# Hybrid decoder block on one core: first feature groups with a pinned first chain, norm products ahead, the prompt's scale and shift on ACT, seven PSUM banks, a third split pair and one group's splits on POOL

## The chip, the core and the metric

The kernel runs on one core of a Trainium2 chip. A core has a matmul engine (TensorE, PE, with its weight loads as PEld), a vector engine (VectorE, DVE), an activation engine (ScalarE, ACT), a general engine (GpSimd, POOL) and a queue engine (SyncE, SP) that issues transfers. The metric is the device time of one execution in microseconds (us); lower is better. A figure for a kernel is the median of its runs.

## The reference

One layer of a decoder for a prompt of 256 tokens and for 8 requests of 4 tokens (288 columns in all), 2048 features wide, in float32:

```python
def block(x, c, st_pool, st_conv, st_ssm, st_ffn, pos0, lp):
    mod = silu(c) @ lp['w_ada'] + lp['b_ada']
    sh1, sc1, g1, sh2, sc2, g2 = split(mod, 6)
    h = rmsnorm(x, lp['norm1']) * (1 + sc1) + sh1
    proj = h @ lp['w_in']
    u_pool, z, xbc, dt_raw = split(proj)
    pool_out, new_pool = pool_mixer(u_pool, st_pool, pos0, lp['pool_w'], lp['pool_scale'])
    ssd_out, new_conv, new_ssm = ssd_mixer(z, xbc, dt_raw, st_conv, st_ssm, ...)
    mix = concatenate([pool_out, ssd_out]) @ lp['w_out']
    x = x + g1 * mix
    h2 = rmsnorm(x, lp['norm2']) * (1 + sc2) + sh2
    ffn_out, new_ffn = conv_ffn(h2, st_ffn, lp['w_up'], lp['ffn_conv_w'], lp['ffn_conv_b'], lp['w_down'])
    return x + g2 * ffn_out, new_pool, new_conv, new_ssm, new_ffn
```

`pool_mixer` averages over trailing windows, `ssd_mixer` is a depthwise convolution and a chunked state-space scan over 24 heads with a gated norm, `conv_ffn` is an MLP of width 5504 whose gate passes a short convolution. The outputs are both sets of tokens and the new states.

## The kernel before

Features lie on the partitions, tokens in the free dimension: a matmul has a 128 by 128 weight block and 288 columns. Each product in float32 is made of three matmuls (`mm3`, lines 235 to 237): weight hi by input hi, weight hi by input lo, weight lo by input hi. All weights stream in as tiles of up to 512 KB. `load` issues one on SP's queue into a slot of the tag "raw", waiting for a free one; `split` makes of it a pair of the tag "wsp": ACT casts the hi part (line 229), and DVE subtracts it from the raw tile for the lo part (line 230). The three rotating lists of slots are kept by `_W`: the pool w1 has RAW1 = 8 raws and SPLIT1 = 2 pairs for the whole kernel, and w0 adds RAW0 = 7 raws until the last feature group starts.

The input projection's 28 output tiles that are needed first (the scan's inputs, two pooling tiles and six tiles of z) are made not in one pass but in six passes over groups of features, since the features get ready one by one:

```python
KGROUPS = [(0, 1), (1, 1), (2, 2), (4, 4), (8, 4), (12, 4)]
```

Group gi has its first k-tile and the number of them. For each group there are three pieces of work. `ada_group_units(gi)` multiplies the conditioning by that group's columns of w_ada (tile adag, line 314, weights raw_ada), in as many visits as `VISIT` says: (raw tiles in a visit, output tiles of the group before at which the visits stand). It transposes the result (adat_g, line 329), adds the bias (ada, DVE, line 339) and makes the multiplier (amul, DVE, line 279). `modulate` makes the normalized input h_g: the product with the reciprocal norm rstd (DVE, line 377), scale and shift of the prompt's 256 columns (DVE, line 380), of the 32 sample columns (POOL, lines 385 and 386), then the hi part h1k by ACT (line 388) and the lo part by DVE (line 389). `xbc_units(gi)` runs the 28 tiles, each with 3 matmuls for every k-tile of the group, in one of 3 PSUM banks of the pool pm, and takes each bank out: group 0 by a copy of ACT (line 588), the later groups by an addition of DVE (line 590) to cvp, upp and ups, or zy. `MOD[gi]` says how many tiles before group gi's end the visits of the next group are finished and its `modulate` stands.

Each engine takes its instructions in the order that the program and its scheduler's priorities give; `split` and `modulate` have a high priority, so their instructions stand ahead of those written around them where nothing pins them. Behind the last group follow the dt product, the rest of the projection (uz, pool and z tiles) beside convolution, scan and norm of the mixer, the other parts of w_ada (adap, line 351), then the output projection, gate, value and down projection of the MLP.

## Time and profile before

| | |
|---|---|
| time, median of 3 runs | 1369.44 us (1365.91 to 1371.44) |
| profiled execution, its own time | 1371.33 us |
| its span | 1369.5 us |
| its mean granted TensorE clock | 0.992 |
| first matmul of groups 0, 1, 2, 3 | 21.77, 37.30, 56.80, 92.42 us |
| first matmul of the dt product, of uz, of the output projection | 202.25, 273.35, 392.24 us |
| DMA, mean over the span | 236 GB/s |

The page of a profile gives for each engine its busy time, share of the span and number of instructions. A row of the timeline has start and duration in us, engine, line, operation, output tile, input tiles and their shapes, the count where equal rows were joined, and in brackets the idle time ahead of it on its engine with what ended it. A row of a grouped view has the total busy time in us and the mean of one in ns. The span is the time between the profile's first and last instruction; the execution's own time is about 1.8 us longer.

### The profile page before, as it was taken

To read this page: it belongs to the slowest core of one execution; us is meant where nothing else is said; L and a number is where in the kernel's file an instruction comes from. 1 tells how busy PE (TensorE), PEld (TensorE's weight loads), DVE (VectorE), ACT (ScalarE), POOL (GpSimd) and SP (SyncE) were. 2 spreads that over 40 slices of the span, in tenths; PEclk is the share of its full clock that TensorE was granted. 3 is DMA by queue.
4 is the path that set the end of the run, shared out by engine and by line. 5 is a ranking of instruction groups with operands and counts; after the bars stand their busy time and mean duration, and the time that the engine had idled before them with its cause. 6 is when DMAs were issued, how large, how long until landed. Compare 5 with 4: busy or idle time off the path is not lost.

```text
span 1369.5 us, 26363 instructions
## 1 busy us (share of the span) xinstructions
PE 1338.9 (98%) x10565; PEld 1249.5 (91%) x10565; DVE 826.8 (60%) x1448; ACT 575.3 (42%) x925; POOL 230.4 (17%) x428
## 2 busy tenths in 40 slices
PE   9899999999989999999999999999999999999997
PEld 7788988777679898988999999999999999999997
DVE  3865667878674448654655455566565566566553
ACT  5322334388643334533443333444343334344442
POOL 0000000222222223111211001222120011122221
PEclk9999999999999999999999999999999999999998
DMA  9898796888878877788555555655555665556531
GB/s 376 344 349 309 270 338 258 299 292 310 306 300 318 314 268 260 239 284 289 198 187 183 162 177 189 197 188 190 186 176 164 188 195 185 192 199 188 185 119 69
DMA packets 97194, 323.20 MB, mean 236 GB/s; under 512 B 10736, under 2 KB 19888, under 8 KB 97072
## 3 DMA queue, kind: packets, MB, share of 16 engines
q1 hardware_dynamic: 93168, 310.63, 65.1%
q0 software_dynamic: 3184, 9.69, 1.9%
q8 instruction: 83, 1.36, 0.4%
q10 hardware_dynamic: 720, 1.19, 0.2%
q14 instruction: 39, 0.32, 0.1%
HBM read 309.78 MB, written 10.39 MB: 234 GB/s over the span
## 4 chain that ended last, share of the span: by engine, by line
PE 90%; DMA 4%; DVE 3%; ACT 1%; issue 0%; POOL 0%; SPq 0%; DVEq 0%; POOLq 0%; ACTq 0%
PE mm_down L236 7%; PE mm_down L237 7%; PE mm_down L235 7%; PE mm_val L236 6%; PE mm_gate L236 6%; PE mm_gate L235 6%; PE mm_gate L237 6%; PE mm_val L237 6%; PE mm_val L235 6%; PE xbc L235 4%; PE adap L351 4%; PE xbc L236 4%; PE xbc L237 4%; PE mm_out L235 3%; PE mm_out L236 2%; PE mm_out L237 2%
## 5 line engine op out<-in xcount | busy, mean ns | idle before, releaser
L236 PE MATMUL mm_down<-ahl,wsp_down 128*128 128x288 f32 x688 | 204.3, 297 | 0.0
L237 PE MATMUL mm_down<-ahl,wsp_down 128*128 128x288 f32 x688 | 202.8, 295 | 0.0
L235 PE MATMUL mm_down<-ahl,wsp_down 128*128 128x288 f32 x688 | 202.1, 294 | 0.0
L236 PE MATMUL mm_val<-h2k,wsp_val 128*128 128x288 f32 x640 | 190.1, 297 | 0.0
L236 PE MATMUL mm_gate<-h2k,wsp_gate 128*128 128x288 f32 x640 | 190.0, 297 | 0.0
L237 PE MATMUL mm_gate<-h2k,wsp_gate 128*128 128x288 f32 x640 | 188.8, 295 | 0.0
L237 PE MATMUL mm_val<-h2k,wsp_val 128*128 128x288 f32 x640 | 188.8, 295 | 0.0
L235 PE MATMUL mm_gate<-h2k,wsp_gate 128*128 128x288 f32 x640 | 188.8, 295 | 0.0
L235 PE MATMUL mm_val<-h2k,wsp_val 128*128 128x288 f32 x640 | 188.0, 294 | 0.0
L230 DVE TENSOR_TENSOR wsp_down<-raw_down,wsp_down 128x1024 fp32r<-128x1024 f32 x96 | 108.0, 1125 | 121.8 <-ACT wsp_down L229 121.8
L230 DVE TENSOR_TENSOR wsp_gate<-raw_gate,wsp_gate 128x1024 fp32r<-128x1024 f32 x80 | 98.1, 1228 | 136.2 <-ACT wsp_gate L229 136.1
L229 ACT CAST wsp_down<-raw_down 128x1024 fp32r<-128x1024 f32 x96 | 92.2, 960 | 167.3 <-PE mm_down L237 116.9
L229 ACT CAST wsp_gate<-raw_gate 128x1024 fp32r<-128x1024 f32 x80 | 83.9, 1050 | 160.4 <-PE mm_gate L237 69.0
L235 PE MATMUL xbc<-h1k,wsp_xbc 128*128 128x288 f32 x448 | 136.4, 306 | 8.9 <-DVE zy L590 4.0
L229 ACT CAST wsp_val<-raw_val 128x1024 fp32r<-128x1024 f32 x80 | 84.1, 1051 | 122.8 <-issue 103.7
L236 PE MATMUL xbc<-h1k,wsp_xbc 128*128 128x288 f32 x448 | 134.4, 300 | 0.9 <-DVE h1k L389 0.9
L237 PE MATMUL xbc<-h1k,wsp_xbc 128*128 128x288 f32 x448 | 132.7, 297 | 0.0
L235 PEld LDWEIGHTS mm_down<-ahl,wsp_down 128*128 128x128 f32 x688 | 129.6, 188 | 0.0
L236 PEld LDWEIGHTS mm_down<-ahl,wsp_down 128*128 128x128 f32 x688 | 129.3, 188 | 0.0
L237 PEld LDWEIGHTS mm_down<-ahl,wsp_down 128*128 128x128 f32 x688 | 129.2, 188 | 0.0
L235 PEld LDWEIGHTS mm_gate<-h2k,wsp_gate 128*128 128x128 f32 x640 | 120.5, 188 | 5.0 <-ACT ahl L1070 4.2
L235 PEld LDWEIGHTS mm_val<-h2k,wsp_val 128*128 128x128 f32 x640 | 120.6, 188 | 0.0
(316 smaller groups left out, 3000.5 us busy)
## 6 DMA issues: line engine op xcount, KB each, us to landing
raw_adap<-wflat SPq DMA_DIRECT2D x128, 512.0 KB, 5.9
raw_gate<-wflat SPq DMA_DIRECT2D x80, 512.0 KB, 3.5
raw_val<-wflat SPq DMA_DIRECT2D x80, 512.0 KB, 3.6
raw_ada<-wflat SPq DMA_DIRECT2D x64, 512.0 KB, 8.0
raw_xbc<-wflat SPq DMA_DIRECT2D x55, 512.0 KB, 8.6
raw_down<-wflat SPq DMA_DIRECT2D x48, 512.0 KB, 3.6
raw_out<-wflat SPq DMA_DIRECT2D x32, 512.0 KB, 6.4
raw_down<-wflat SPq DMA_DIRECT2D x32, 384.0 KB, 3.1
```

The costliest lines, as they stand in the source:

```text
L229: nc.scalar.copy(hi[:, :n], raw[:, a:a + n])
L230: nc.vector.tensor_tensor(lo[:, :n], raw[:, a:a + n], hi[:, :n].bitcast(F32), ALU.subtract)
L235: nc.tensor.matmul(ps, whi[:, w], bh, start=first, stop=False)
L236: nc.tensor.matmul(ps, whi[:, w], bl, start=False, stop=False)
L237: nc.tensor.matmul(ps, wlo[:, w], bh, start=False, stop=last)
L351: i = nc.tensor.matmul(ps[32 * j:32 * j + 32, :512], sc_c[:, k, :], raw[:, (j % 2) * 512:(j % 2) * 512 + 512], start=(k == ay - 1), stop=( ...
```

## The change

Eight things are changed together. (1) In group 0 the chain to the first h (line 339's add to line 389's lo part) is pinned in program order, and the split of the first xbc tile is written ahead of it; the second tile's split is written behind it, pinned as well. (2) The products with the norm are made in place on the x tiles, ahead: k-tile 0 and k-tiles 1 to 3 before the first chain, the other twelve in three instructions at tiles 4, 10 and 16 of group 0 (`normalize`). (3) `modulate1` makes the sample columns on DVE and the prompt's scale and shift with one ACT instruction for each k-tile. (4) In groups 0 to 4, four of every seven output tiles (m % 7 > 2) use a bank of the pool behind `aux`, which has four, so that the tiles run through seven banks. (5) In group 0 four of the 28 tiles (m % 7 == 5) are taken out by DVE. (6) RAW1 goes from 8 to 10 and RAW0 from 7 to 5, and w0 has a pair, so that there are three pairs until the last group starts; the raws are 15 as before until then, and 10 instead of 8 after it. (7) In group 1 POOL makes the lo parts of the splits. (8) Visits of group 3 come in four fours rather than two eights, MOD of groups 0 and 1 goes from 4 and 5 to 10 and 8, the load of vec moves from group 1 to group 3, and the scratch memory of DMAs with software descriptors is halved to 8192 bytes.

```diff
@@ -36,13 +36,13 @@
-RAW1, RAW2 = 8, 1
-RAW0 = 7
+RAW1, RAW2 = 10, 1
+RAW0, SPLIT0 = 5, 1
 SPLIT1, SPLIT2 = 2, 2
-PHASE = (192, 32, 0)
+PHASE = (192, 32, 0, 128)
 YK = 2
-VISIT = {1: (4, (10,)), 2: (4, (7, 15)), 3: (8, (8, 19)), 4: (8, (8, 19)), 5: (8, (8, 19))}
-MOD = (4, 5, 6, 6, 6)
+VISIT = {1: (4, (10,)), 2: (4, (7, 15)), 3: (4, (4, 9, 14, 19)), 4: (8, (8, 19)), 5: (8, (8, 19))}
+MOD = (10, 8, 6, 6, 6)
@@ -222,13 +222,24 @@
-    def split(raw, a, n, name):
+    kpo = tc.keep_in_program_order
+
+    def split(raw, a, n, name, eng=None, pin=False):
         pair = wp[0].tile([P, 2 * RAWC + 64], F32R, tag="wsp", name="wsp_" + name)
         hi, lo = pair[:, 0:RAWC], pair[:, RAWC + 32:2 * RAWC + 32]
         with tc.high_priority():
-            nc.scalar.copy(hi[:, :n], raw[:, a:a + n])
-            nc.vector.tensor_tensor(lo[:, :n], raw[:, a:a + n], hi[:, :n].bitcast(F32), ALU.subtract)
+            i = nc.scalar.copy(hi[:, :n], raw[:, a:a + n])
+            j = (eng or nc.vector).tensor_tensor(lo[:, :n], raw[:, a:a + n], hi[:, :n].bitcast(F32), ALU.subtract)
+        if pin:
+            kpo(i)
+            kpo(j)
         return hi, lo
+
+    def split_xbc(gi, ci, pin=False):
+        (ks, ms), key = _xbc_chunks(gi)[ci], ("xbc", gi, ci)
+        return ready.pop(key, None) or split(load(key), 0, len(ms) * len(ks) * P, f"xbc{gi}_{ci}",
+                                             nc.gpsimd if gi == 1 else None, pin)
+
 
     def mm3(ps, whi, wlo, c, bh, bl, first, last, n=P):
         w = slice(c * n, c * n + n)
...
@@ -323,8 +334,11 @@
             if gi:
                 yield
         r = 32 * nj
+        pin = kpo if gi == 0 else (lambda i: i)
+        if gi == 0:
+            ready[("xbc", 0, 0)] = split_xbc(0, 0, True)
         if gk == 1:
-            asb = ada_sb(ps, nb, f"g{gi}")
+            asb = ada_sb(ps, nb, f"g{gi}", pin=pin)
             pt = aux(f"adat_g{gi}")
             nc.tensor.matmul(pt[:, :r], asb[:, :nb], early[:, K_S2:K_S2 + r], start=True, stop=True)
             if gi == 0:
@@ -336,8 +350,8 @@
             o = ada[:, 0:2, k0:k0 + gk, :].rearrange("p a (b i) c -> p a b i c", b=nj // 2)[:, :, :, i, :]
             b = bada[:, 0:2, k0:k0 + gk].rearrange("p a (b i) -> p a b i", b=nj // 2)[:, :, :, i]
             src = pt[:, i * r:(i + 1) * r].rearrange("p (a b c) -> p a b c", a=2, b=nj // 2)[:, :, :, 0:NC9]
-            nc.vector.tensor_tensor(o, src, b.unsqueeze(3).to_broadcast([P, 2, nj // 2, NC9]), ALU.add)
-        ada_scale(0, 1, early[:, V_N1:V_N1 + KT], k0, gk)
+            pin(nc.vector.tensor_tensor(o, src, b.unsqueeze(3).to_broadcast([P, 2, nj // 2, NC9]), ALU.add))
+        pin(ada_scale(0, 1, early[:, V_N1:V_N1 + KT], k0, gk))
 
     def ada_part_units(part, ay=1):
         ps = pa.tile([P, 512], F32, tag="ada", name=f"adap{part}")
@@ -387,6 +401,29 @@
         for i in range(gk):
+
+    def normalize(k0, gk, r):
+        xv = xav(k0, gk)
+        kpo(nc.vector.tensor_tensor(xv, xv, r.unsqueeze(1).to_broadcast([P, gk, N]), ALU.mult))
+
+    def modulate1(k0, gk, name):
+
+        h = kp.tile([P, 4, N], F32, tag="hmod", name="h_" + name, bufs=2)
+        xv = xav(k0, gk)
+        pin = kpo if k0 == 0 else (lambda i: i)
+        with tc.high_priority():
+            hs = h[:, :gk, NP:N].rearrange("p k (b l) -> p k b l", b=NB)
+            xs = xv[:, :, NP:N].rearrange("p k (b l) -> p k b l", b=NB)
+            sa = amul[:, 0, k0:k0 + gk, 1:NC9].unsqueeze(3).to_broadcast([P, gk, NB, NL])
+            sb = ada[:, 0, k0:k0 + gk, 1:NC9].unsqueeze(3).to_broadcast([P, gk, NB, NL])
+            pin(nc.vector.tensor_tensor(hs, xs, sa, ALU.mult))
+            pin(nc.vector.tensor_tensor(hs, hs, sb, ALU.add))
+            for i in range(gk):
+                pin(nc.scalar.activation(h[:, i, 0:NP], xv[:, i, 0:NP], AF.Identity,
+                                         scale=amul[:, 0, k0 + i, 0:1], bias=ada[:, 0, k0 + i, 0:1]))
+                pin(nc.scalar.copy(xhi[0][k0 + i], h[:, i, :]))
+                pin(nc.vector.tensor_tensor(xlo[0][k0 + i], h[:, i, :], xhi[0][k0 + i].bitcast(F32), ALU.subtract))
 
 
     class _W:
@@ -569,9 +606,10 @@
     def xbc_units(gi):
         k0, gk = KGROUPS[gi]
         for ci, (ks, ms) in enumerate(_xbc_chunks(gi)):
-            hi, lo = split(load(("xbc", gi, ci)), 0, len(ms) * gk * P, f"xbc{gi}_{ci}")
+            hi, lo = split_xbc(gi, ci)
             for b, m in enumerate(ms):
-                ps = pm.tile([P, 512], F32, tag="mm", name=f"xbc{gi}_{m}")
+                wide = gi < len(KGROUPS) - 1 and m % 7 > 2
+                ps = aux(f"xbc{gi}_{m}") if wide else pm.tile([P, 512], F32, tag="mm", name=f"xbc{gi}_{m}")
                 for i, k in enumerate(ks):
@@ -584,7 +622,9 @@
                 for o, v in parts:
-                    if gi == 0:
+                    if gi == 0 and m % 7 == 5:
+                        nc.vector.tensor_copy(o, v)
+                    elif gi == 0:
                         nc.scalar.copy(o, v)
                     else:
                         nc.vector.tensor_tensor(o, o, v, ALU.add)
@@ -843,10 +883,14 @@
     adas = chain(*(ada_part_units(p, AY) for p in (2, 3, 4)))
+    normalize(0, 1, rstd1p)
+    normalize(1, 3, rstd1p)
     drain(ada_group_units(0))
     w0 = w0_ctx.enter_context(tc.tile_pool(name="w0", bufs=1, reuse_waits="tile"))
-    wp[0].add(w0, RAW0, 0)
-    modulate(xav(0, KGROUPS[0][1]), rstd1p, 0, 0, 0, KGROUPS[0][1], "g0")
+    shift(w0, PHASE[3], "v")
+    wp[0].add(w0, RAW0, SPLIT0)
+    modulate1(0, 1, "g0")
+    ready[("xbc", 0, 1)] = split_xbc(0, 1, True)
@@ -895,7 +939,7 @@
-            if gi == 1:
+            if gi == 3:
                 nc.sync.dma_start(vec, ins["vec"])
             if gi == 4:
                 late_loads()
@@ -903,11 +947,13 @@
             k0, gk = KGROUPS[gi + 1]
         for i, m in enumerate(xbc_units(gi)):
             if not last:
+                if gi == 0 and i in (4, 10, 16):
+                    normalize(4 + 4 * ((i - 4) // 6), 4, rstd1)
                 if i in VISIT[gi + 1][1]:
                     next(nxt)
                 if i == ET - MOD[gi]:
                     drain(nxt)
-                    modulate(xav(k0, gk), rstd1, 0, 0, k0, gk, f"g{gi + 1}")
+                    modulate1(k0, gk, f"g{gi + 1}")
@@ -1277,7 +1323,7 @@
 
 def kernel(**inputs):
     ins = _layout(inputs)
-    nc = _bacc.Bacc("TRN2", target_bir_lowering=False, num_devices=1)
+    nc = _bacc.Bacc("TRN2", target_bir_lowering=False, num_devices=1, dynamic_dma_scratch_size=8192)
```

Where the change moves instructions is shown by the orders of each engine. First DVE, from its first norm product to the first h1k lo part: h_g is the modulated input, xa the x tile, wsp_xbc_0 the pair of the first weight tile. Before:

```order
L377 TENSOR_TENSOR h_g_256<-xa_90,pbrstd_155 128x288
L377 TENSOR_TENSOR h_g_477<-xa_90,rstd_159 128x288
L339 TENSOR_TENSOR ada<-adat_g_243,early 128x2x9
L279 SCALAR_TENSOR_TENSOR amul<-ada,early 128x9
L380 TENSOR_SCALAR h_g_256<-h_g_256,amul,ada 128x256
L230 TENSOR_TENSOR wsp_xbc_0_265<-raw_xbc_0_263,wsp_xbc_0_265 128x1024
L389 TENSOR_TENSOR h1k_172<-h_g_256,h1k_172 128x288
```

And with the change:

```order
L408 TENSOR_TENSOR xa_90<-xa_90,pbrstd_155 128x288
L408 TENSOR_TENSOR xa_90<-xa_90,pbrstd_155 128x864
L232 TENSOR_TENSOR wsp_xbc_0_245<-raw_xbc_0_243,wsp_xbc_0_245 128x1024
L353 TENSOR_TENSOR ada<-adat_g_250,early 128x2x9
L290 SCALAR_TENSOR_TENSOR amul<-ada,early 128x9
L420 TENSOR_TENSOR h_g_264<-xa_90,amul 128x32
L421 TENSOR_TENSOR h_g_264<-h_g_264,ada 128x32
L426 TENSOR_TENSOR h1k_172<-h_g_264,h1k_172 128x288
```

The split of the first weight tile has moved from behind the prompt's product to ahead of the bias add, the norm product of k-tile 1 has become one for k-tiles 1 to 3, and in place of the prompt's product stand two of the 32 sample columns.

Next DVE again, near the end of group 1, around group 2's bias add: ada and amul are the bias add and the multiplier of group 2, wsp_xbc_0 and wsp_xbc_1 there are group 2's first two pairs. Before:

```order
L339 TENSOR_TENSOR ada<-adat_g_740,early 128x2x18
L590 TENSOR_TENSOR zy_192<-zy_192,xbc_24_759 128x288
L230 TENSOR_TENSOR wsp_xbc_0_781<-raw_xbc_0_779,wsp_xbc_0_781 128x1024
L279 SCALAR_TENSOR_TENSOR amul<-ada,early 128x18
L590 TENSOR_TENSOR zy_193<-zy_193,xbc_25_764 128x288
L380 TENSOR_SCALAR h_g_744<-h_g_744,amul,ada 128x256
L230 TENSOR_TENSOR wsp_xbc_1_822<-raw_xbc_1_820,wsp_xbc_1_822 128x1024
L380 TENSOR_SCALAR h_g_744<-h_g_744,amul,ada 128x256
L389 TENSOR_TENSOR h1k_174<-h_g_744,h1k_174 128x288
L590 TENSOR_TENSOR zy_193<-zy_193,xbc_26_769 128x288
L389 TENSOR_TENSOR h1k_175<-h_g_744,h1k_175 128x288
```

And with the change, from the second split of group 2 on:

```order
L232 TENSOR_TENSOR wsp_xbc_1_824<-raw_xbc_1_822,wsp_xbc_1_824 128x1024
L630 TENSOR_TENSOR cvp_164<-cvp_164,xbc_19_713 128x8x4
L630 TENSOR_TENSOR upp<-upp,xbc_20_719 128x256
L630 TENSOR_TENSOR ups<-ups,xbc_20_719 128x8x4
L353 TENSOR_TENSOR ada<-adat_g_727,early 128x2x18
L630 TENSOR_TENSOR upp<-upp,xbc_21_740 128x256
L290 SCALAR_TENSOR_TENSOR amul<-ada,early 128x18
L630 TENSOR_TENSOR ups<-ups,xbc_21_740 128x8x4
L420 TENSOR_TENSOR h_g_731<-xa_90,amul 128x2x32
L630 TENSOR_TENSOR zy_192<-zy_192,xbc_22_746 128x288
L421 TENSOR_TENSOR h_g_731<-h_g_731,ada 128x2x32
L630 TENSOR_TENSOR zy_192<-zy_192,xbc_23_751 128x288
```

The second split of group 2 has moved from behind the multiplier to ahead of the bias add (the first stands four rows above the piece that is shown), the sample products (lines 420 and 421) have come in where the prompt's stood, and the chain begins at the upp tiles rather than between the zy tiles.

Last POOL, from its first tile instruction on; wsp_xbc_0 to wsp_xbc_3 are the four weight tiles of group 1. Before:

```order
L385 TENSOR_TENSOR h_g_256<-h_g_256,amul 128x32
L386 TENSOR_TENSOR h_g_256<-h_g_256,ada 128x32
L385 TENSOR_TENSOR h_g_477<-h_g_477,amul 128x32
L386 TENSOR_TENSOR h_g_477<-h_g_477,ada 128x32
L385 TENSOR_TENSOR h_g_744<-h_g_744,amul 128x2x32
L386 TENSOR_TENSOR h_g_744<-h_g_744,ada 128x2x32
```

And with the change:

```order
L232 TENSOR_TENSOR wsp_xbc_0_505<-raw_xbc_0_503,wsp_xbc_0_505 128x1024
L232 TENSOR_TENSOR wsp_xbc_1_599<-raw_xbc_1_597,wsp_xbc_1_599 128x1024
L232 TENSOR_TENSOR wsp_xbc_2_692<-raw_xbc_2_690,wsp_xbc_2_692 128x1024
L232 TENSOR_TENSOR wsp_xbc_3_758<-raw_xbc_3_756,wsp_xbc_3_758 128x512
L516 COPY cvp_161<-st 128x5x8x3
```

The sample products have left POOL, and the four lo parts of group 1 stand in their place, ahead of the copies of the state.

6 lines of the change are left out of this document (3 added, 3 removed).

## The prediction

> **What bounds the kernel now.** I read the page first, then the table of stretches cut at the starts of the feature groups, then TensorE's waits.
>
> ```profile
> PE 1338.9 (98%) x10565; PEld 1249.5 (91%) x10565; DVE 826.8 (60%) x1448; ACT 575.3 (42%) x925; POOL 230.4 (17%) x428
> ```
>
> TensorE is busy 98%, so the change can win only where it stands, or where its clock drops. A stretch's columns are us, then busy time (and instructions) of PE, weight loads, DVE, ACT and POOL, then granted clock, DMA share, GB/s.
>
> ```profile
> 21.77:37.30 15.53, 15.00 (x151) 13.53 (x151) 7.91 (x13) 14.30 (x55) 0.65 (x2) 1.00 1.03 407
> 37.30:56.80 19.50, 16.91 (x215) 15.15 (x213) 17.01 (x57) 6.00 (x9) 0.62 (x2) 1.00 1.03 407
> 56.80:92.42 35.62, 31.64 (x293) 27.23 (x293) 26.13 (x72) 8.63 (x12) 0.94 (x2) 0.95 0.82 307
> 92.42:145.05 52.63, 51.22 (x448) 47.45 (x449) 33.12 (x75) 16.40 (x19) 2.53 (x7) 0.97 0.86 333
> 145.05:202.25 57.20, 57.20 (x506) 52.02 (x507) 34.98 (x79) 15.86 (x19) 1.07 (x3) 1.00 0.80 283
> 273.35:392.24 118.89, 113.45 (x953) 85.14 (x949) 86.30 (x158) 86.83 (x193) 29.23 (x39) 0.99 0.79 289
> 800.00:1200.00 400.00, 400.00 (x3030) 400.00 (x3030) 232.93 (x340) 156.66 (x219) 67.51 (x144) 1.00 0.58 186
> ```
>
> The last row gives the price of a matmul of 288 columns: 400/3030 = 0.132 us. With it each group gets a floor. The MLP is at its floor; the first rows are groups 0 to 4, and there ACT (14.30 of 15.53) and then DVE (17.01 of 19.50) are the fuller engines. The waits (us in total, times, longest):
>
> ```profile
> PE xbc L235 <- DVE zy L590: 4.0, 2, 2.6
> PE adap L351 <- DMA raw_adap<-wflat: 3.5, 2, 2.8
> PE xbc L235 <- ACT h1k L388: 3.4, 2, 2.1
> ```
>
> The waits are short, but four of the longest are followed by some 3.4 us at half clock, two of them in groups 2 and 3:
>
> ```profile
> 57.60:61.20 3.60, 3.09 (x13) 3.09 (x14) 3.39 (x9) 0.43 (x1) 0.00 (x0) 0.55 1.02 409
> 91.70:95.30 3.60, 2.88 (x12) 2.88 (x13) 2.66 (x5) 0.99 (x1) 0.00 (x0) 0.55 1.03 420
> 378.40:382.00 3.60, 3.60 (x21) 3.43 (x17) 1.48 (x3) 1.58 (x4) 0.05 (x1) 0.55 0.91 354
> 395.50:399.10 3.60, 3.60 (x17) 0.94 (x18) 3.60 (x15) 3.27 (x9) 0.00 (x0) 0.55 0.91 319
> ```
>
> Mean clock 0.55 over 3.6 us means 0.45 × 3.6 = 1.6 us of work lost each time, on top of the wait. The Trainium skill ("TensorE: Matmul & The Clock Gate", Part 1) has the clock halve after at least one idle window of about 3.4 us. Here it halves behind waits of 1.9 to 2.8 us, all shorter than that, so the rows decide. By the rule the wait that I leave in C below would bring no half clock; by the rows it can, and D would then be 1.7 us smaller.
>
> **The change part by part.** Sums are on the profiled execution's own time, 1371.33 us; the median of the three runs, 1369.44, lies 1.9 lower.
>
> A, the first chain. Rows run from the DVE's prompt product to the first matmul; the lines after them are a POOL add in group 0 and ACT's scale-and-bias operation at the kernel's end.
>
> ```profile
> 19.56 0.41 DVE L380 TENSOR_SCALAR h_g<-h_g,amul,ada 128x256 f32<-128x256 f32 x1
> 19.70 0.37 POOL L385 TENSOR_TENSOR h_g<-h_g,amul 128x32 f32<-128x32 f32 x1 [19.25 <-ACT wsp_xbc L229]
> 19.88 1.27 DVE L230 TENSOR_TENSOR wsp_xbc<-raw_xbc,wsp_xbc 128x1024 fp32r<-128x1024 f32 x1
> 20.15 1.10 POOL L386 TENSOR_TENSOR h_g<-h_g,ada 128x32 f32<-128x32 f32 x1
> 21.28 0.43 ACT L388 CAST h1k<-h_g 128x288 fp32r<-128x288 f32 x1 [1.73 <-POOL h_g L386]
> 21.77 0.40 PE L235 MATMUL xbc<-h1k,wsp_xbc 128*128 128x288 f32 x1 [1.27 <-ACT h1k L388]
> ...
> 33.42 0.24 POOL L386 TENSOR_TENSOR h_g<-h_g,ada 128x32 f32<-128x32 f32 x1
> ...
> L1124 ACT ACTIVATE xf<-x,vec 128x288 f32<-128x288 f32 x16 | 8.3, 521 | 0.0
> ```
>
> POOL's add takes 1.10 us beside DVE's split and 0.24 later: the chain waits for that. The change puts the split ahead of the chain, two small products on DVE and the prompt on ACT. From 19.56: ACT's product 0.52, its cast 0.43, and the 0.06 from cast to matmul that 21.28 + 0.43 to 21.77 shows, gives about 20.6. **A = −1.1** (−1.6 if ACT starts at once, 0 if the split ahead is late by as much).
>
> B, group 0. ACT empties all 28 banks:
>
> ```profile
> 22.82 5.74 ACT L588 COPY cvp<-xbc 128x256 f32<-128x256 f32 x28 [0.16 <-PE xbc L237]
> ...
> 28.14 1.95 PE L314 MATMUL adag<-raw_ada,sc_c 128*32 128x128 f32 x64
> ```
>
> 28 copies are 14 tiles, so 0.41 us a tile. Four tiles go to DVE: 4 × 0.41 = 1.6 off ACT's 15.5. TensorE's floor is 28 × 3 × 0.132 + 1.95 (one visit) = 13.0, so **B = −1.6** (0 if ACT's casts come late, −2.5 at the floor). Wide banks (seven in place of three) let TensorE run ahead of a copy and have no price.
>
> C, group 1 and the wait behind it. The rows at its end:
>
> ```profile
> 54.13 1.23 DVE L230 TENSOR_TENSOR wsp_xbc<-raw_xbc,wsp_xbc 128x1024 fp32r<-128x1024 f32 x1 [0.16 <-ACT wsp_xbc L229]
> 56.05 1.32 DVE L230 TENSOR_TENSOR wsp_xbc<-raw_xbc,wsp_xbc 128x1024 fp32r<-128x1024 f32 x1
> 56.32 0.43 ACT L388 CAST h1k<-h_g 128x288 fp32r<-128x288 f32 x1 [0.54 <-POOL h_g L386]
> 56.80 0.40 PE L235 MATMUL xbc<-h1k,wsp_xbc 128*128 128x288 f32 x1 [2.11 <-ACT h1k L388]
> 58.11 0.61 PE L236 MATMUL xbc<-h1k,wsp_xbc 128*128 128x288 f32 x1 [0.91 <-DVE h1k L389]
> ```
>
> Two splits of group 2 lie across the chain that makes group 2's h. DVE was busy 17.01 us; 3.5 splits at 1.23 (4.3 us) go to POOL, so DVE needs 12.7, below TensorE's floor of 28 × 3 × 0.132 + 2 × 1.95 = 15.0, and the chain is put at tile 20 rather than 23. But the two splits of group 2 stay on DVE, ahead of the chain. I keep a wait of 2.8 of the 3.0 (2.11 + 0.91): 15.0 + 2.8 = 17.8, **C = −1.7**; −4.5 if the wait goes, 0 if POOL's lo parts are late. What does a split take on POOL? No row shows one. The nearest:
>
> ```profile
> L836 POOL TENSOR_TENSOR zy<-zy,rstdy 128x864 f32<-128x864 f32 x1 | 2.1, 2056 | 4.1 <-ACT rstdy L213 4.1
> L767 POOL TENSOR_TENSOR ssq<-ssq,ysq 128x288 f32<-128x288 f32 x11 | 11.6, 1054 | 56.6 <-ACT ysq L763 56.6
> ```
>
> Scaled to 1024 elements, 2.4 us (2056 × 1024/864) to 3.7 (1054 × 1024/288); I take 2.4, the row nearest in size. TensorE uses a pair for 8 × 3 × 0.132 = 3.2 us, and the third pair lets POOL work one pair ahead, so even 3.7 plus ACT's 1.05 fits in two of those. Does POOL hold DVE's accumulations up? Copies of st by POOL ran beside them:
>
> ```profile
> 129.21 0.51 DVE L590 TENSOR_TENSOR cvp<-cvp,xbc 128x256 f32<-128x256 f32 x2
> 129.87 1.00 POOL L479 COPY cvp<-st 128x120 f32<-128x120 f32 x4 [41.28 <-DMA st<-st]
> 130.14 0.53 DVE L590 TENSOR_TENSOR cvp<-cvp,xbc 128x256 f32<-128x256 f32 x2 [0.41 <-PE xbc L237]
> ```
>
> 0.53 beside POOL, 0.51 alone: no. "SBUF — State Buffer" of the Trainium skill ("Who interferes with whom") says that a DVE instruction with two SBUF inputs contends with a POOL instruction that reads SBUF, and one with at most one does not. The accumulations have one input in PSUM, and the rows agree; DVE's lo and sample products have two, so by the rule C could give back one POOL split, 2.4 us.
>
> D, group 2. Its floor is 28 × 2 × 3 × 0.132 + 2 × 3.66:
>
> ```profile
> 80.23 3.66 PE L314 MATMUL adag<-raw_ada,sc_c 128*32 128x256 f32 x64
> ```
>
> That is 22.2 + 7.3 = 29.5 against 35.62. Over the floor stand the 0.91 above, a half clock of 1.6, a wait of up to 2.6 for the bank that DVE empties (zy), and about 1.0 of small waits. The visits in fours free the raw slots earlier, and seven banks cover the chain of group 3, so **D = −5.5**; −3.8 if the half clock stays, and 0 only if the bank wait merely moves, which seven banks speak against.
>
> E, groups 3 and 4. The half clock at 91.70 is gone if D's wait is (1.6, shared between the groups), and the other wait for zy (4.0 − 2.6 = 1.4) with seven banks. **E = −2.5** (0 to −3.0).
>
> F, the middle. After group 4 the loads have 10 raw slots rather than 8.
>
> ```profile
> 382.75 9.05 SPq L222 DMA_DIRECT2D raw_adap<-wflat x3
> 395.48 1.58 PE L351 MATMUL adap<-raw_adap,sc_c 128*32 128x512 f32 x5 [2.84 <-DMA raw_adap<-wflat]
> 377.69 0.31 PE L748 MATMUL y<-e,xdt 128*64 128x32 f32 x4 [1.89 <-DVE e L735]
> ```
>
> Three issues stretch over 9.05 us while SP waits for slots, and TensorE then waits 2.84 for a late tile. Two more slots should take this wait and its half clock (2.84 + 1.6 = 4.4). The 1.89 for e stands behind a split; it may go or move. Moving the start also reshuffles ready times, so I count **F = −3.6** between 0 and −8 (both waits with a half clock each). The moved vec load is one transfer on SP, now ahead of group 3's tiles, which wait in slots by then; DVE first reads it in group 3. The sample products that leave POOL, the norm products (the same elements, now in group 0) and the new pinning have DVE's spare 15.5 − 7.9 us as cover; without it they would cost up to three products ahead of group 1.
>
> Sum: −1.1 − 1.6 − 1.7 − 5.5 − 2.5 − 3.6 = −16.0, so 1371.33 − 16.0 = 1355.3, and 1353.4 on the median's scale; I take **1355**.
>
> **The rivals.** First, the middle gives back. There TensorE stood only 5.4 of 118.89 us, and weights come at 289 GB/s against 407 in groups 0 and 1, so bytes are no bound; but where the serial work of DVE and ACT ends late, an earlier start buys new waits. One such wait of 2 us with its half clock costs 3.6, two cost 7.2, and F would be 0: −12.4 + 3.6 = −8.8 or −12.4 + 7.2 = −5.2, that is 1362.5 to 1366. For it: two such waits stand there now. Against: the slots.
>
> Second, POOL is late. At 3.7 a split and blocked against DVE's lo products, group 1 loses C, and D keeps its half clock: −16.0 + 1.7 + 1.7 = −12.6, about 1359.
>
> Third, the early part does not do what it says: the two splits of group 2 still hold the chain, the waits and both half clocks stay, and D, E and F are nothing: −1.1 − 1.6 − 1.7 = −4.4, about 1367.
>
> Fourth, slower. The software DMAs' scratch is halved. POOL issues these, and its copies for the gate's convolution queue behind them. The page's 17% for POOL speaks against a queue there.
>
> ```profile
> L1108 POOL DMA_DIRECT2D o_ssms<-hst x16 | 12.0, 752 | 83.3 <-DVE hst L1107 83.1 <-issue 0.2
> ```
>
> If each of the 16 then held POOL past the slack of one projection (48 × 0.132 = 6.3 us), and each overrun by 2 us reached TensorE, 32 us would come on top: 1355 + 32 = 1387. It decides from a hold of 6.3 us, eight times an issue's 0.75 now.
>
> **How the numbers follow.** Forecast (1349 to 1360) 0.57; first rival 0.18; second 0.12; third 0.08; fourth 0.05. 0.5% of 1369.44 is 6.8 us, about what a measurement of this kernel can tell from no change, so faster means below 1362.6. That holds the forecast, the second rival and 0.10 of the first, where one wait comes: 0.79. Same: the 0.08 of the first with two waits, and the third: 0.16. Slower: 0.05. The range 1348 to 1366 runs from F at its −8 with C's wait gone in part, (1371.33 − 12.4 − 8 − 2.8), up to the end of the first rival; the third and the fourth, 0.13, and a tail of the forecast stay out.
>
> **What would show it.** A: first xbc matmul near 20.6. B, C: group 1 starting near 34.5, group 2 near 52.3. D, E: no clock below 1.0 in the groups, group 3 starting near 82 and the dt matmuls near 190. POOL: splits of 2.4 us, DVE's accumulations unchanged. F: no wait of adap for its raw tile near 380. It is wrong if group 2 starts above 56, if half clocks stay in groups 2 and 3, if the dt matmuls come 12 us earlier but the out projection does not, or if POOL's issues lengthen.

## The result and the profile after

The changed kernel takes 1359.6 us (median of 5 runs, 1355.82 to 1360.36), the kernel before 1369.94 (5 runs, 1365.91 to 1371.44): a ratio of 0.9918, 95% interval 0.9895 to 0.9942. The gain is 10.3 us, 0.8%; the forecast was 14.4 (1355 against the 1369.44 of three runs), its range 1348 to 1366. The profiled execution took 1360.36 us with a span of 1358.6, 10.9 below the span before.

The page's first part, and the stretches between the same points of the program as before: groups 0 to 4, from the dt product to uz, uz to the output projection, that to its last matmul, and on to the first matmul of up.

```profile
PE 1336.0 (98%) x10565; PEld 1249.9 (92%) x10565; DVE 819.6 (60%) x1446; ACT 580.0 (43%) x934; POOL 228.1 (17%) x420
...
20.52:34.67 14.15, 13.68 (x151) 13.08 (x151) 11.12 (x19) 12.41 (x48) 2.40 (x1) 1.00 1.03 408
34.67:53.56 18.89, 16.89 (x215) 15.43 (x213) 13.86 (x55) 7.26 (x14) 6.05 (x3) 0.94 1.03 406
53.56:85.75 32.19, 31.59 (x300) 27.00 (x299) 21.93 (x64) 10.49 (x16) 0.00 (x0) 0.98 1.02 402
85.75:138.17 52.42, 52.24 (x469) 48.45 (x468) 35.58 (x82) 18.70 (x25) 1.54 (x5) 1.00 0.86 331
138.17:190.09 51.92, 51.92 (x468) 48.34 (x467) 31.77 (x74) 17.75 (x23) 0.14 (x1) 1.00 0.71 270
190.09:263.07 72.98, 72.98 (x559) 57.62 (x556) 59.64 (x141) 31.28 (x44) 11.94 (x23) 1.00 0.87 319
263.07:377.94 114.87, 112.68 (x952) 85.05 (x948) 83.52 (x153) 84.81 (x190) 28.42 (x36) 0.99 0.79 295
377.94:500.93 122.99, 119.80 (x900) 108.12 (x900) 60.41 (x98) 45.71 (x65) 27.48 (x37) 0.97 0.82 307
500.93:509.69 8.76, 6.25 (x53) 2.41 (x53) 3.70 (x11) 2.36 (x6) 1.07 (x4) 1.00 0.78 275
```

The same stretches of the kernel before that the prediction does not show, from the dt product to uz, the output projection, and on to up:

```profile
202.25:273.35 71.10, 71.10 (x543) 57.10 (x540) 58.90 (x135) 30.39 (x42) 10.27 (x20) 1.00 0.78 284
...
392.24:513.82 121.58, 118.74 (x900) 105.94 (x900) 60.56 (x97) 45.42 (x64) 28.37 (x37) 0.99 0.84 312
513.82:521.07 7.25, 6.25 (x54) 2.41 (x53) 2.77 (x9) 2.42 (x7) 1.20 (x4) 1.00 0.69 238
```

| stretch | before | after | measured | forecast |
|---|---|---|---|---|
| A, to the first xbc matmul | 21.77 | 20.52 | −1.25 | −1.1 |
| B, group 0 | 15.53 | 14.15 | −1.38 | −1.6 |
| C, group 1 | 19.50 | 18.89 | −0.61 | −1.7 |
| D, group 2 | 35.62 | 32.19 | −3.43 | −5.5 |
| E, groups 3 and 4 | 109.83 | 104.34 | −5.49 | −2.5 |
| sum at the dt product | 202.25 | 190.09 | −12.16 | −12.4 |
| F, from there to the end | 1167.2 | 1168.5 | +1.3 | −3.6 |

By this table the sum at the dt product came out, its parts less well, and all of the loss lies behind it. But one number needs care: group 3's and 4's stretches hold 17 matmuls fewer than before (448 + 506 against 469 + 468), and the stretch to uz 16 more, 1.88 us longer. One adap visit of 16 matmuls, ahead of the dt product before, now stands behind it. Without it E is −3.6, the sum at the dt product −10.3, and F −0.6. So the close agreement of −12.16 and −12.4 is partly luck: of the 5.1 us that are missing on the forecast's −16.0, 2.1 were lost ahead of the dt product and 3.0 behind it.

TensorE's waits, in the form of before (us in total, times, longest). pout is the result of a pooling tile, h2k the normalized input of the MLP, and ysum, made from ssq, a sum for the mixer's norm:

```profile
PE pool L855 <- DVE pout L850: 3.2, 1, 3.2
PE mm_up L246 <- ACT h2k L402: 2.5, 1, 2.5
PE xbc L246 <- DVE cvp L630: 2.0, 2, 1.4
PE ysum L197 <- POOL ssq L807: 1.2, 1, 1.2
```

The four waits that stood at the head of the list before (for zy, adap, h1k, and e) have gone from its head. In their place stand one for pout at the head of the output projection, one for h2k ahead of the up projection (1.0 before), and two for a bank in group 1.

### The profile page after: what moved, and what is told of

Its sections match the earlier page's. It is cut to its first block, busy times and chain, and to the rows that moved or that the text cites. A ratio compares the mean times of both kernels' runs of the same rounds, so it can differ in the third digit from the quotient of the medians.

```text
span 1358.6 us, 26335 instructions
## 1 busy us (share of the span) xinstructions
PE 1336.0 (98%) x10565; PEld 1249.9 (92%) x10565; DVE 819.6 (60%) x1446; ACT 580.0 (43%) x934; POOL 228.1 (17%) x420
## 4 chain that ended last, share of the span: by engine, by line
PE 95%; DVE 2%; DMA 1%; ACT 1%; issue 0%; POOL 0%; DVEq 0%; POOLq 0%; ACTq 0%
PE mm_down L247 7%; PE mm_down L248 7%; PE mm_down L246 7%; PE mm_val L247 6%; PE mm_gate L247 6%; PE mm_gate L246 6%; PE mm_gate L248 6%; PE mm_val L248 6%; PE mm_val L246 6%; PE xbc L246 4%; PE xbc L247 4%; PE xbc L248 4%; PE adap L365 4%; PE mm_out L246 3%; PE mm_out L247 3%; PE mm_out L248 3%
## 5 line engine op out<-in xcount | busy, mean ns | idle before, releaser
L246 PE MATMUL xbc<-h1k,wsp_xbc 128*128 128x288 f32 x448 | 133.5, 302 | 2.7 <-DVE cvp L630 2.0
L247 PE MATMUL xbc<-h1k,wsp_xbc 128*128 128x288 f32 x448 | 133.1, 298 | 0.2 <-DVE h1k L426 0.2
L248 PE MATMUL xbc<-h1k,wsp_xbc 128*128 128x288 f32 x448 | 130.9, 296 | 0.6 <-DVE wsp_xbc L232 0.6
```

The costliest lines, as they stand in the source:

```text
L246: nc.tensor.matmul(ps, whi[:, w], bh, start=first, stop=False)
L247: nc.tensor.matmul(ps, whi[:, w], bl, start=False, stop=False)
L248: nc.tensor.matmul(ps, wlo[:, w], bh, start=False, stop=last)
```

## The experiments

Eleven kernels were run, in three sets. Where a start is given it is TensorE's first matmul of that stretch in the profiled execution. The first conditioning matmul comes at 12.72 to 13.48 us in the thirteen profiled executions, so a difference of starts below 0.8 us shows nothing. A ratio is to the kernel before, run in the same set (1370.18, 1369.33 and 1371.44 us there).

**Four parts taken back, one at a time.** First group 1's lo parts on DVE:

```diff
-                                             nc.gpsimd if gi == 1 else None, pin)
+                                             None, pin)
```

> The changed kernel with group 1's lo parts back on DVE. If DVE is what holds group 1, it gets 3.5 x 1.23 = 4.3 us back, and group 2 starts at 55.5 to 57.5 us (53.56 with the change), the total 2 to 4 us above 1359.6. If only the two splits of group 2 hold group 1's end, group 2 starts within 0.5 us of 53.56.

It took 1354.98 us (ratio 0.9892, 0.9861 to 0.9924), not slower than the changed kernel. Group 2 started at 53.88, 0.3 us later, and the dt product at 188.96, 1.1 earlier. The 4.3 us on DVE were not what held group 1, which took 19.31 us in place of 18.89:

```profile
34.57:53.88 19.31, 16.19 (x213) 14.86 (x214) 16.97 (x59) 6.80 (x12) 0.00 (x0) 1.00 1.03 405
```

The row of what did, in the changed kernel, with the two matmuls that wait (idle 0.58 and 1.41 us, and 0.88 and 1.71 from the start of the matmul before):

```profile
49.22 0.37 PE L246 MATMUL xbc<-h1k,wsp_xbc 128*128 128x288 f32 x1 [0.58 <-DVE cvp L630]
49.79 1.23 DVE L232 TENSOR_TENSOR wsp_xbc<-raw_xbc,wsp_xbc 128x1024 fp32r<-128x1024 f32 x1 [0.39 <-ACT wsp_xbc L231]
51.26 0.40 PE L246 MATMUL xbc<-h1k,wsp_xbc 128*128 128x288 f32 x1 [1.41 <-DVE cvp L630]
```

Those are group 2's splits. They stand among group 1's additions as before, only earlier, and TensorE waits for the banks that the additions behind them would free. Group 2's bias add stands behind them too (51.46 us), so they hold the chain of group 2's h as well.

Second, three banks for all groups:

```diff
-                wide = gi < len(KGROUPS) - 1 and m % 7 > 2
+                wide = False
```

> The changed kernel with three PSUM banks for all groups. If the banks removed the waits for DVE's zy additions, these come back: groups 2 to 4 together take 139 to 141 us (136.5 with the change: 53.56 to 190.09), with a half clock again, and the total is 3 to 5 us higher. If the visits and the earlier chain did it, groups 2 to 4 stay within 0.5 us of 136.5.

1360.77 us (0.9932, 0.9909 to 0.9954). Its groups 0 and 1, and groups 2 to 4 in one stretch:

```profile
20.44:36.51 16.07, 15.02 (x150) 13.50 (x151) 10.09 (x19) 13.91 (x49) 2.38 (x1) 1.00 1.03 408
36.51:57.08 20.57, 18.97 (x248) 16.20 (x246) 15.73 (x58) 7.03 (x11) 6.03 (x3) 1.00 1.03 406
57.08:195.37 138.29, 134.65 (x1200) 123.60 (x1199) 88.48 (x215) 46.93 (x62) 2.67 (x6) 0.99 0.82 315
```

Groups 2 to 4 lost 1.8 us against 136.53, and a visit of 32 matmuls (1.83, half of the 3.66 for 64) has moved from there into group 1, whose 1.7 us more are that visit. So the banks are worth 3.6 us in groups 2 to 4, as expected, and 1.9 in group 0, where I had given them no price: it took 16.07 us although DVE took its four tiles. Of the 5.3 us at the dt product only 1.2 were left at the end of the kernel: the stretches behind it were shorter by as much, and no part of them was undone by this edit. Most of that is TensorE's clock: behind the dt product and up to 1330 us the changed kernel's profile has 10.24 us at half clock, and this one 3.41, which is 3.4 us of work.

Third, the visits and the place of the chain:

```diff
-VISIT = {1: (4, (10,)), 2: (4, (7, 15)), 3: (4, (4, 9, 14, 19)), 4: (8, (8, 19)), 5: (8, (8, 19))}
-MOD = (10, 8, 6, 6, 6)
+VISIT = {1: (4, (10,)), 2: (4, (7, 15)), 3: (8, (8, 19)), 4: (8, (8, 19)), 5: (8, (8, 19))}
+MOD = (4, 5, 6, 6, 6)
```

> The changed kernel with VISIT of group 3 and MOD of before. If the smaller visits and the earlier chain carry group 1 and 2, group 2 starts 1 to 3 us later than 53.56 and takes 33.5 to 35 us (32.2 with the change), with a DMA share under 0.95 there (1.02 with the change). If the banks and the third pair carry it, both stay within 0.5 us.

1364.08 us (0.9958, 0.994 to 0.9976). Group 2 started at 56.84 (3.3 later) and the dt product at 196.90 (6.8 later): the largest loss of the four. Group 2 took 33.8 us at a DMA share of 0.78, both as expected if the visits carry it, but 1.8 of that is the wait for the next h: up to its last matmul it took 31.98 us as against 32.06. The loss sits in the waits between the groups, 1.1, 2.8 and 1.8 us from the start of one matmul to the next, and in the half clock behind them (10.24 us ahead of the dt product, 3.41 in the changed kernel: 3.4 us of work), and not in a slower stream of weights.

Fourth, the raw slots of before:

```diff
-RAW1, RAW2 = 10, 1
-RAW0, SPLIT0 = 5, 1
+RAW1, RAW2 = 8, 1
+RAW0, SPLIT0 = 7, 1
```

> The changed kernel with RAW1 = 8 and RAW0 = 7, so that the raw slots are those of before; all else stays. My theory: the dt product starts at 190.1 within 0.5 us; the wait for a late adap tile comes back, and the waits for pout (3.2) and h2k (2.5) go or shrink, so that the up projection starts within 2 us of 509.7 and the total is within 2 us of 1359.6: two more slots bring nothing. The rival, that the slots bring what I counted in F: the up projection starts 3 us later or more, at 512.7 or above.

1358.56 us (0.9917, 0.9888 to 0.9947): no slower. The dt product began at 189.88 and up at 506.87, 2.8 us earlier than with ten slots. So the total came out as the theory had it. That two more slots bring nothing is not shown by it: this profile has 3.41 us at half clock between the first xbc matmul and 1330 us, the changed kernel's 13.65, and the later pair with the lo parts on DVE leans the other way (0.9892 with ten slots, 0.9918 with eight, the intervals overlapping). One step of the theory failed: no wait for an adap tile came back. With eight slots the scheduler orders the head of the output projection in another way, too.

**Three waits taken away.** Both splits of group 2 on POOL, those of group 1 on DVE:

```diff
-                                             nc.gpsimd if gi == 1 else None, pin)
+                                             nc.gpsimd if gi == 2 and ci < 2 else None, pin)
```

> The changed kernel with the lo parts of group 1 on DVE and those of group 2's first two tiles on POOL instead. If DVE's two splits of group 2 hold the banks at group 1's end, the waits of 0.88 and 1.71 us near 50 us and their half clock go: group 2 starts at 50 to 51.5 us (53.56 with the change, 53.88 with all of group 1 and 2 on DVE), and the dt product at 186 to 188 (190.09). If POOL's 2.4 us for a lo part is too late for group 2's first matmuls, or the weights' arrival sets the pace, group 2 starts above 53 us.

1355.79 us (0.9901, 0.9874 to 0.9928). The two waits for banks went, and group 1 took 15.4 us from its first to its last matmul, near the floor of 15.0. But group 2 started at 53.22. TensorE waited 2.55 us there, 2.84 from the start of the matmul before. The rows at that place:

```profile
50.22 2.35 POOL L232 TENSOR_TENSOR wsp_xbc<-raw_xbc,wsp_xbc 128x1024 fp32r<-128x1024 f32 x1 [0.90 <-ACT wsp_xbc L231]
50.56 2.09 DVE L421 TENSOR_TENSOR h_g<-h_g,ada 128x64 f32<-128x64 f32 x1
52.74 0.76 ACT L425 CAST h1k<-h_g 128x288 fp32r<-128x288 f32 x2 [1.59 <-DVE h_g L421]
53.22 0.40 PE L246 MATMUL xbc<-h1k,wsp_xbc 128*128 128x288 f32 x1 [2.55 <-ACT h1k L425]
```

In the changed kernel the same addition of the sample columns takes 0.22:

```profile
52.60 0.22 DVE L421 TENSOR_TENSOR h_g<-h_g,ada 128x64 f32<-128x64 f32 x1
```

It ends here when POOL's split does. A small operation with two inputs in SBUF waited out a POOL instruction of 2.35 us, and the chain with it. This is the mechanism that the rows of the first chain showed the other way round, POOL waiting for DVE.

The last pooling tile's steps at high priority:

```diff
-    for gn in late.values():
-        drain(gn)
+    with tc.high_priority():
+        for gn in late.values():
+            drain(gn)
```

> The changed kernel with the last pooling tile's steps at high priority, so that pout's additions stand ahead of the bias adds and of the first mixk lo part on DVE. If TensorE's wait of 3.2 us near 380 us is one for DVE's order, it shrinks by about 1.1 us (0.49 for the bias adds, 0.5 for one lo part), and the output projection ends 1 us earlier after its start than the 122.99 us of the change. If the wait hangs on something else (the projection's upp tile, POOL), it stays at 3.2 us.

1355.85 us (0.9902, 0.9872 to 0.9932). The wait for pout fell from 3.2 to 2.2 us, as expected, and the output projection took 120.79 in place of 122.99. The additional 1.2 us is TensorE's clock, and not shown to be the edit's: 0.99 over that stretch, where the changed kernel's row above has 0.97.

```profile
PE pool L855 <- DVE pout L850: 2.2, 1, 2.2
...
376.18:496.97 120.79, 118.64 (x900) 106.92 (x900) 60.83 (x98) 45.69 (x65) 27.50 (x37) 0.99 0.83 313
```

The third and fourth up splits pinned:

```diff
-            hi, lo = ready.pop(("upk", k), None) or split(load(("upk", k)), 0, 2 * FK * P, f"upk{k}")
+            hi, lo = ready.pop(("upk", k), None) or split(load(("upk", k)), 0, 2 * FK * P, f"upk{k}", None, k < 4)
```

> The changed kernel with the splits of the third and fourth up tile pinned in program order, behind ACT's copy of the norm. If ACT's cast that waits for its transfer holds the norm's copy, the stretch from the end of the output projection to the up projection goes from 8.76 us back to 7.2 to 7.6 (7.25 before the change), and the total is 1 to 1.5 us lower. If the norm waits for something else, it stays at 8.76 within 0.3 us.

1357.57 us (0.9914, 0.9889 to 0.9939). The stretch ahead of up took 6.62 us, below the 7.25 of before. The rows of the changed kernel that this undoes, ACT's cast of an up tile and the norm's copy behind it, and then the first matmul of up:

```profile
506.20 0.83 ACT L231 CAST wsp_upk<-raw_upk 128x768 fp32r<-128x768 f32 x1 [2.36 <-DMA raw_upk<-wflat]
506.94 0.39 ACT L213 COPY rstd<-pbrstd 128x288 f32<-128x288 f32 x1
509.69 0.53 PE L246 MATMUL mm_up<-h2k,wsp_upk 128*128 128x288 f32 x2 [2.51 <-ACT h2k L402]
```

The cast stood 2.36 us for its transfer, with the norm ready and queued behind it. In the profiles of all six kernels with ten slots and without the pin the cast stands ahead of the norm's copy, and this stretch takes 7.5 to 8.8 us; in the five with eight slots it stands behind it, and the stretch takes 6.7 to 7.3.

**Two undone together, two alone, and the waits together.** The slots of before and the lo parts on DVE, both edits as above:

> The changed kernel with the raw slots of before and group 1's lo parts on DVE, both undone together. If both bring nothing or cost a little, as each alone did (1354.98 and 1358.56), the dt product starts at 188.5 to 190.5, and the total lies at 1353 to 1357. If they need each other, it lies above 1359.6.

1357.74 us (0.9918, 0.9889 to 0.9947), just outside what was expected, and not above 1359.6. The dt product began at 189.65. They do not need each other. With the lo parts on DVE in both, eight slots come out above ten (0.9918 against 0.9892), where alone they did not.

The kernel before with VISIT[3] and MOD of the change, and nothing else:

> The kernel before with VISIT of group 3 and MOD of the change, and nothing else of it. Taking these back from the changed kernel moved the dt product by 6.8 us. If they act by themselves, it starts at 194 to 197 us here (202.25 before). If they need the banks and the sample products on DVE, it starts above 199.

1371.71 us against 1371.44 (1.0007, 0.9997 to 1.0016): nothing. Group 2 started at 61.16 and the dt product at 206.00, later than before. The waits fit an earlier chain that, with three banks, takes DVE's time from additions that TensorE waits for: those for zy rose from 4.0 us in 2 to 6.3 in 4, and the one for an adap tile from 3.5 to 6.8.

```profile
PE adap L351 <- DMA raw_adap<-wflat: 6.8, 2, 5.6
PE xbc L235 <- DVE zy L590: 6.3, 4, 2.7
```

The kernel before with seven banks, and nothing else:

```diff
-                ps = pm.tile([P, 512], F32, tag="mm", name=f"xbc{gi}_{m}")
+                wide = gi < len(KGROUPS) - 1 and m % 7 > 2
+                ps = aux(f"xbc{gi}_{m}") if wide else pm.tile([P, 512], F32, tag="mm", name=f"xbc{gi}_{m}")
```

> The kernel before with seven PSUM banks for groups 0 to 4, and nothing else of the change. Taking the banks back from the changed kernel moved the dt product by 5.3 us, 3.5 of it in groups 0 and 1. If they act by themselves, it starts at 196 to 198 us here (202.25 before). If ACT's copies set group 0 and DVE's splits group 1 whatever the banks, it starts above 200.

1361.69 us (0.9926, 0.9911 to 0.9942): nearly the ratio of the whole change. The dt product started at 193.67, 8.6 of the change's 12.2 us; in both, 1.9 of it is the adap visit that now stands behind the dt product (1230 matmuls here, 1246 before). Groups 2 to 4 before, and groups 0, 1 and 2 to 4 here:

```profile
56.80:202.25 145.45, 140.05 (x1246) 126.70 (x1247) 94.23 (x224) 40.89 (x50) 4.54 (x12) 0.98 0.83 307
```

```profile
21.92:37.06 15.14, 13.62 (x150) 13.01 (x150) 6.57 (x12) 13.30 (x54) 1.62 (x2) 1.00 1.03 407
37.06:56.76 19.70, 15.91 (x213) 14.72 (x214) 18.50 (x60) 6.21 (x11) 0.62 (x2) 0.97 1.03 407
56.76:193.67 136.91, 136.91 (x1230) 126.02 (x1231) 92.64 (x222) 40.67 (x50) 4.55 (x12) 0.98 0.83 315
```

TensorE is busy all of the 136.91 us: not one wait for zy is left, with everything else as it was but that visit. Group 0's tiles take 13.32 us from first to last (15.14 less the 1.82 of waiting for the next h) with all 28 copies on ACT.

Last, the edits that took waits away in one kernel: the pooling steps and the up splits as above, and for the splits

```diff
-                                             nc.gpsimd if gi == 1 else None, pin)
+                                             nc.gpsimd if (gi, ci) == (2, 0) else None, pin or (gi, ci) == (2, 1))
```

> The changed kernel with four edits: group 1's lo parts on DVE, of group 2 the first on POOL and the second on DVE pinned behind the chain, the last pooling tile's steps at high priority, the third and fourth up splits pinned. In the run with both splits of group 2 on POOL, DVE's sample add stood 2.09 us in place of 0.22 beside POOL's second split, and TensorE waited 2.84 us; with POOL idle by then I expect 0.22 again, group 2's start at 50.5 to 51.5 us and the dt product at 185.5 to 187.5; the wait for pout 2.2 and the stretch from the out to the up projection 6.6 to 7.4, as each edit alone gave. Total 1350 to 1354, below the change's 1359.6. If the half clock or a new wait takes what is won, the total lies at 1355 to 1358 as in each edit alone.

1350.59 us (0.985, 0.9833 to 0.9866), better than both kernels: 20.9 us below the kernel before, and the interval lies clear of the changed kernel's. DVE's sample addition is short again (0.22 us), and group 2 started at 51.55, just behind what was expected, the dt product at 186.67, and up at 500.40, 9.3 us ahead of the changed kernel.

```profile
35.02:51.55 16.53, 15.70 (x213) 14.73 (x213) 14.63 (x57) 6.71 (x12) 2.41 (x1) 1.00 1.03 406
51.55:186.67 135.12, 134.94 (x1230) 123.14 (x1231) 90.57 (x219) 46.94 (x63) 1.68 (x6) 1.00 0.86 334
186.67:500.40 313.73, 309.01 (x2451) 250.49 (x2448) 205.50 (x398) 162.56 (x301) 68.99 (x99) 0.99 0.83 308
```

Group 1 fell from 18.89 to 16.53, and groups 2 to 4 have no half clock.

## Why the prediction was right, and where it was wrong

The time lies in the range and the sign is right. The first sum, −12.16 against −12.4 at the dt product, is partly luck, since 1.88 of it is the visit that only moved. Of the signs that were to show the forecast, the first xbc matmul, POOL's splits, the start of the dt product and the missing wait for an adap tile came; group 2 at 53.56 rather than 52.3, group 3 at 85.75 rather than 82, and a half clock from 51.46 to 54.87 did not fit. Point by point:

**A** was right in size and cause. From the matmul of adat_g, the tile that the bias add reads, to the first xbc matmul it took 3.11 us before (18.66 to 21.77) and 2.07 now (18.45 to 20.52), so −1.04; the other 0.2 us is the earlier start of this execution. The split ended ahead of the chain, the sample addition took 0.19 us, and the first matmul came at 20.52 (20.6 forecast).

**B** was right in size and wrong in cause. The step was "ACT empties all 28 banks", and so four tiles on DVE were to be the gain, with the banks at no price. Seven banks with all 28 tiles on ACT gave a group 0 of 13.32 us; four tiles on DVE with three banks gave 16.07. So what held group 0 was TensorE and ACT taking turns at three banks, though ACT was busy 14.30 of 15.53 us; in the run with seven banks it had 11.87 busy of the 13.32. Whether the four tiles on DVE add anything behind seven banks no run shows.

**C** failed at the step "3.5 splits at 1.23 go to POOL". That step was worth nothing (group 2 starts 0.3 us later without it). The two splits of group 2, which I had left in the sum as a wait of 2.8 us, moved ahead of the chain, cost 0.88 and 1.71 us at the banks, and held the chain itself. A half clock followed (0.94 over the group), which I had allowed only for D, but it cost group 1 nothing: in the run with the pooling steps moved up, the same program up to there, the clock stays at 1.00 and group 2 still starts 33.09 us after the first xbc matmul, as against 33.04; TensorE waits 0.85 us for h1k instead. POOL's time was as estimated, 2.40 us for a full tile:

```profile
L232 POOL TENSOR_TENSOR wsp_xbc<-raw_xbc,wsp_xbc 128x1024 fp32r<-128x1024 f32 x3 | 7.2, 2403 | 35.7 <-ACT wsp_xbc L231 35.7
```

**D and E** are best read together: −8.92, or −7.0 without the visit that moved, against −8.0. The reason given, banks that take away the waits for zy, is the one that seven banks alone showed. That the visits were smoother gave group 2 nothing of its own; with MOD they pay only behind seven banks, as the pair of runs shows (nothing alone, 6.8 us at the dt product when taken back, 3.4 of it half clock). That D came out 2.1 us short and E, without that visit, 1.1 over is a further piece of luck for their sum.

**F** is the term that was wrong: −3.6 forecast, +1.3 measured, −0.6 without the visit. "Two more slots should take this wait and its half clock" failed in its second half. The wait of 2.84 for an adap tile did go, but it had covered another. The pooling matmul needs pout, and DVE has pout ready 5.3 us after the output projection's first matmul in both kernels. In the kernel before the late visit ended after that (the matmul came 6.49 us after the first), in the changed one it ends 3.2 us ahead of it (5.44 us). Before:

```profile
392.24 0.40 PE L235 MATMUL mm_out<-mixk,wsp_out 128*128 128x288 f32 x1
397.37 0.16 DVE L810 TENSOR_TENSOR pout<-pout,upp 128x16 f32<-128x16 f32 x1
398.73 1.00 PE L815 MATMUL pool<-pout,poolw 128*128 128x288 f32 x2
```

And with the change:

```profile
377.94 0.40 PE L246 MATMUL mm_out<-mixk,wsp_out 128*128 128x288 f32 x1
383.08 0.16 DVE L850 TENSOR_TENSOR pout<-pout,upp 128x16 f32<-128x16 f32 x1
383.38 1.30 PE L855 MATMUL pool<-pout,poolw 128*128 128x288 f32 x2 [3.19 <-DVE pout L850]
```

So 1.05 of the 4.4 us were to be had. The run with the pooling steps moved up shows that it is DVE's order that makes pout late: 3.2 became 2.2. In that order there is also a split that takes 2.60 us beside POOL's product of 2.05 at 373.18 (2.61 before), where the splits of xbc tiles take 1.23; how much of that reaches pout no run shows.

```profile
373.70 2.60 DVE L232 TENSOR_TENSOR wsp_out<-raw_out,wsp_out 128x1024 fp32r<-128x1024 f32 x1
```

With ten slots ACT's cast of an up tile came to stand ahead of the norm's copy, 1.5 us between the output projection and up, which pinning took back. The half clock did not go either: from the output projection's first matmul to up it lasts 3.41 us before and 6.83 with the change, 1.7 us of work more. Those two outweigh the 1.05: over that stretch the kernel lost 2.9 us (131.75, and 128.83 before), 0.8 of which these three leave unexplained. From the dt product to the output projection it had won 2.1, or 4.0 without the visit.

Of the rivals, the first, new waits in the middle, names what took the loss behind the dt product, but it had F at +3.6 or +7.2 us; the measured +1.3 (−0.6 without the visit) lies between it and the forecast. The third, that group 2's splits still hold the end of group 1, was right for that one place. The second did not occur in the form that I gave it, and that its time of about 1359 is the measured one is chance: POOL was in time, and DVE's additions did not slow: in group 1, where POOL's splits stand, those of 256 columns take 413 ns in the mean, and 419 before. The sentence on the Trainium skill's "SBUF — State Buffer" ("Who interferes with whom") gave the right price of what came when POOL's split met a DVE operation with two SBUF inputs, one POOL split: 2.09 us instead of 0.22, in an experiment and not in the change's own splits on POOL. The fourth rival is out: the issues that go through the halved scratch take 752 ns as before.

```profile
L1154 POOL DMA_DIRECT2D o_ssms<-hst x16 | 12.0, 752 | 82.8 <-DVE hst L1153 82.6 <-issue 0.2
```

How much of the 2 to 4 us between kernels that differ in one edit is the edit, and how much the places of the half clock? Span times mean granted clock, averaged over a kernel's executions, leaves the time lost at lower clock out. It is an estimate from the runs' clocks, good to perhaps 1 us, since TensorE would have waited in part of that time anyway.

| kernel | time, us | span times clock, us |
|---|---|---|
| before (three sets) | 1369.3 to 1371.4 | 1358.2 to 1359.0 |
| changed | 1359.60 | 1347.9 |
| group 1's lo parts on DVE | 1354.98 | 1346.3 |
| three banks | 1360.77 | 1353.0 |
| visits and MOD of before | 1364.08 | 1349.3 |
| eight slots | 1358.56 | 1350.4 |
| eight slots, lo parts on DVE | 1357.74 | 1349.0 |
| before with seven banks | 1361.69 | 1350.3 |
| four edits together | 1350.59 | 1343.6 |

By this estimate the banks are worth 5 us in the changed kernel, as the dt product had it, and not the 1.2 of the totals; the ten slots about 2.5 in both pairs; visits and MOD 1.4, with most of what their return cost in time being half clock; and POOL's splits nothing, or less.

What stays open: no run takes back alone the norm products ahead, ACT's scale and shift with the sample columns on DVE, the four tiles on DVE, the third pair, the vec load, the halved scratch, or the gap of 128 bytes that the diff puts ahead of w0 (`PHASE[3]`).

## What to carry to other kernels

An engine that is 92% busy beside a matmul engine need not be the bound: look first at how many banks lie between the two. Here ACT made the same 28 copies in 13.32 us behind seven banks and in 15.53 behind three. More banks do not cover everything: two splits in DVE's queue still cost 0.88 and 1.71 us with seven. Ahead of taking a wait away, read what else is ready only when it ends; a late load here hid a late vector chain. A high priority puts a step ahead on every engine that it uses: a cast that has to wait for its transfer holds what is queued behind it, so steps that are needed later are better pinned behind the short chain.

## What was not expected of the hardware

The half clock does not follow from the length of a wait alone. The same wait of 1.2 us ahead of ysum (ssq) is followed by 3.4 us at 0.69 in the changed kernel and at 1.00 in the run with the pooling steps moved up:

```profile
367.60:371.00 3.40, 3.39 (x19) 3.39 (x20) 1.78 (x9) 0.72 (x3) 0.00 (x0) 0.69 1.02 412
```

```profile
367.40:370.80 3.40, 3.40 (x28) 3.40 (x28) 1.76 (x9) 1.33 (x3) 0.00 (x0) 1.00 1.01 407
```

And the wait of 2.55 us ahead of group 2 in the run with both splits on POOL was followed by none over groups 2 to 4:

```profile
53.22:188.44 135.22, 135.04 (x1230) 123.26 (x1231) 89.11 (x219) 46.96 (x63) 1.67 (x6) 1.00 0.85 330
```

The granted clock in the traces shows what decides. From the first xbc matmul to 1330 us it is 1.00 or 0.50 and nothing between; a mean such as 0.69 mixes the two. The half clock lasts 3.41 us or twice that, and within one execution its stretches start whole steps of 3.413 us apart: in the kernel before at 57.93, 92.06, 378.79 and 395.85, which is 10, 84 and 5 steps. Cut at these steps, the feature groups of the thirteen profiled executions have eleven windows of 3.41 us at full clock with TensorE busy for 1.74 us or less, and a half clock follows each of them; none follows a full-clock window with 1.89 us or more. So a wait counts by how much of it falls into one window. In the changed kernel the two waits for banks in group 1 lie in the window from 48.05 to 51.46, with TensorE busy 1.41 us, and the half clock comes. In the run with the pooling steps moved up the same two waits lie in two windows, with 2.82 and 1.99 busy, and it stays away. The wait of 2.55 us above is cut at 52.05 (2.03 and 2.24 busy), and the wait for ysum lies whole in one window in the changed kernel (2.20 busy) and is cut in the other run (2.53 and 3.08).

Behind the groups busy time alone does not decide: eight executions have the window with 2.20 us around the six matmuls of one column for ysum, and the half clock followed in five of them. Where the steps lie against the program's start differs from one execution to the next, so a wait of this length costs a half clock partly by chance.

The Trainium skill ("TensorE: Matmul & The Clock Gate", Part 1) has windows that run freely, whatever the kernel does; that would let the same wait count in one execution and not in the next, and the steps and rows above agree. That a window must be idle for all of its 3.4 us they do not bear out: one with 1.74 us busy was enough.
